# Placing the DVE and ACT code of a softmax kernel at the start of a 128-instruction block

## The chip, the cores and the metric

The kernel runs on one core of one Trainium2 chip. The metric is the device time of one execution in microseconds (us), given as the median of several. The *span* of a profile, from the first to the last instruction of the core, is 1.8 to 1.9 us shorter than that time. Engines: DVE is VectorE, ACT is ScalarE, POOL is GpSimd, PE is TensorE, SP is SyncE.

## The reference

A softmax with a temperature over rows of 1024 numbers, 32 x 512 of them, in float32:

```python
def reference(x, temperature):                     # x: 32 x 512 x 1024, temperature 0.5
    scaled = x / temperature
    shifted = scaled - np.max(scaled, axis=-1, keepdims=True)
    exp_x = np.exp(shifted)
    return (exp_x / np.sum(exp_x, axis=-1, keepdims=True)).astype(np.float32)
```

67.11 MB are read and 67.11 MB written.

## The kernel before

Sixteen tiles of 4 MB (128 partitions x 8 rows) pass through six buffers, in place. SP issues the loads, ACT the stores. A tile is worked on in two groups of four rows: DVE takes the maximum, ACT the exponential with the sum, DVE the reciprocal and four multiplications.

```python
TILES = [[8]] * 16
BUFS = 6
GROUP = 4
...
    def load():
        ...
            nc.sync.dma_start(out=xt, in_=dram(xf, i))
    def maximum(g):
        ...
        nc.vector.tensor_reduce(out=top, in_=tiles[i][:, a : a + k, :], ..., op=extreme)
        nc.vector.tensor_scalar_mul(bias, in0=top, scalar1=-scale)
    def exponential(g):
        ...
        for b in range(k):
            nc.scalar.activation(..., Exp, bias=bias[:, b : b + 1], scale=scale,
                                 accum_out=sums[:, b : b + 1])
    def divide(g):
        ...
        nc.vector.reciprocal(recip, sums)
        for b in range(k):
            nc.vector.tensor_scalar_mul(...)
    def store(g):
        ...
            nc.scalar.dma_start(out=dram(of, i)[:, a : a + k, :], in_=...)
...
    with tc.manual_schedule():
        for _ in range(BUFS):
            load()
        for g in range(len(groups) + 1):
            if g < len(groups):
                maximum(g)
                exponential(g)
            if g > 0:
                divide(g - 1)
                store(g - 1)
```

## Time and profile before

| | before |
|---|---|
| time, median (lowest to highest) | 318.26 us (317.97 to 318.32) in the first three runs |
| span of the profile | 316.0 us |
| DVE, ACT busy | 235.5 us, 149.6 us |
| loads, stores: share of the 16 DMA engines' time | 49.7%, 49.2% |
| instruction packets after the first load | 4, of 8192 bytes |

The prediction below reads the main views. Two notes help to follow it. First, the profile shows an engine's instructions being brought in by DMA, as a queue of kind "instruction" (q14 here, with the four packets of 8192 bytes of the table). In the DMA view of a short window, each line of which gives queue, packets, MB and share of the 16 engines' time, a fetch of instructions can be found by narrowing the window. This is the kernel before from 60 to 70 us, and then from 236 to 242 us:

```profile
q10 hardware_dynamic: 73, 2.39, 55.4%
q1 hardware_dynamic: 79, 2.06, 48.5%
q14 instruction: 2, 0.02, 0.4%
...
q10 hardware_dynamic: 47, 1.54, 59.4%
q1 hardware_dynamic: 43, 1.05, 41.1%
q14 instruction: 1, 0.01, 0.3%
```

The two data queues fill the DMA engines (103.9% and 100.5% in these windows); the instruction packets, few and small, stand in the same line as they do.

Second, the trace holds a record of each DMA packet with its start and duration, though not with the DMA engine that moved it. The engine can be recovered: under load a packet starts 3 to 4 ns before the recorded end of the one before it on the same engine, so the packets can be joined into 16 chains. This is worked out from the trace and not a view of the profile. A few chains can't be told apart where two packets end within some nanoseconds; I name a chain's end below only where the chain has its full 256 data packets, 128 loads and 128 stores. Here is one fetch of the kernel before in its chain (start and end in us from the span's start):

```
store packet  63.781 to 64.994   1.213 us
instructions  64.991 to 65.300   0.309 us   (8192 bytes)
load packet   65.297 to 66.972   1.675 us   (an ordinary one takes 1.213)
```

### The profile page before, as it was taken

What the parts mean: (1) busy time and instruction counts of PE and PEld (TensorE: products, weight loads), DVE (VectorE), ACT (ScalarE), POOL (GpSimd) and SP (SyncE); (2) the same over time, 40 slices, a digit from 0 to 9 for tenths busy, and PEclk for the clock granted to TensorE, in tenths of its full rate; (3) what the DMA queues carried; (4) which work ended last, traced back from release to release, by engine and by line L of the source; (5) the groups of instructions that cost most, each with busy time, mean ns of one, the idle gap of its engine ahead of it and who ended that gap; (6) DMA issues with size and microseconds to landing.
All of it is one profiled execution on the core that took longest, in us unless ns stands there. A gap on an engine that the chain in (4) does not pass through costs nothing.

```text
span 316.0 us, 620 instructions
## 1 busy us (share of the span) xinstructions
DVE 235.5 (75%) x224; ACT 149.6 (47%) x257; POOL 0.2 (0%) x4
## 2 busy tenths in 40 slices
DVE  0399999999689494994949859497693976949720
ACT  0176666666526255361554605546064560645500
POOL 0000000000000000000000000000000000000000
DMA  8999999999999999999999999999999999999996
GB/s 332 411 452 423 373 460 415 452 425 431 436 427 440 427 444 423 444 419 448 415 452 411 452 408 456 423 444 427 436 431 432 440 423 444 419 444 419 452 411 274
DMA packets 4612, 134.25 MB, mean 425 GB/s; under 512 B 512, under 2 KB 512, under 8 KB 512
## 3 DMA queue, kind: packets, MB, share of 16 engines
q1 hardware_dynamic: 2304, 67.11, 49.7%
q10 hardware_dynamic: 2304, 67.11, 49.2%
q14 instruction: 4, 0.03, 0.0%
HBM read 67.11 MB, written 67.11 MB: 425 GB/s over the span
## 4 chain that ended last, share of the span: by engine, by line
DVE 49%; DMA 32%; another core or an unknown queue 9%; ACT 5%; issue 1%; DVEq 0%; SPq 0%
DVE top L70 29%; DMA xt<-in_x_dram 20%; DVE xt L93 18%; DMA out_dram<-xt 12%; ACT xt L79 5%; DVE recip L91 1%; DVE bias L73 1%; DVEq L147 0%; SPq L61 0%
## 5 line engine op out<-in xcount | busy, mean ns | idle before, releaser
L79 ACT ACTIVATE xt<-xt,bias 128x1024 f32<-128x1024 f32 x128 | 145.4, 1137 | 136.8 <-DVE recip L91 119.4
L70 DVE TENSOR_REDUCE top<-xt 128x4 f32<-128x4096 f32 x32 | 141.3, 4416 | 62.6 <-DMA xt<-in_x_dram 62.6
L93 DVE TENSOR_SCALAR xt<-xt,recip 128x1024 f32<-128x1024 f32 x128 | 87.7, 749 | 1.1
L79 ACT ACTIVATION_READ_ACCUMULATOR xt<-xt,bias 128x1 f32 x128 | 23.9, 187 | 0.0
L79 ACT ACT_TABLE_LOAD x1 | 1.3, 1283 | 13.0 <-DMA xt<-in_x_dram 13.0
L91 DVE RECIPROCAL recip<-sums 128x4 f32<-128x4 f32 x32 | 5.5, 171 | 2.1 <-ACT xt L79 2.1
L73 DVE TENSOR_SCALAR bias<-top 128x4 f32<-128x4 f32 x32 | 5.4, 170 | 1.1
L133 POOL MEMSET const-bfloat16-1.0<- 128x1 bf16 x1 | 0.1, 101 | 0.0
L133 POOL MEMSET const-uint8-127<- 128x1 uint8 x1 | 0.1, 101 | 0.0
L133 POOL MEMSET const-float32-0.0<- 128x1 f32 x1 | 0.1, 98 | 0.2 <-issue 0.2
L133 POOL MEMSET const-float32-1.0<- 128x1 f32 x1 | 0.1, 98 | 0.0
## 6 DMA issues: line engine op xcount, KB each, us to landing
xt<-in_x_dram SPq DMA_DIRECT2D x16, 4096.0 KB, 50.2
out_dram<-xt ACTq DMA_DIRECT2D x16, 4096.0 KB, 38.6
```

Source lines behind the costliest of these rows:

```text
L70: nc.vector.tensor_reduce(out=top, in_=tiles[i][:, a : a + k, :], axis=mybir.AxisListType.X, op=extreme)
L73: nc.vector.tensor_scalar_mul(bias, in0=top, scalar1=-scale)
L79: nc.scalar.activation(tiles[i][:, a + b, :], tiles[i][:, a + b, :], mybir.ActivationFunctionType.Exp, bias=bias[:, b : b + 1], scale=scal ...
L91: nc.vector.reciprocal(recip, sums)
L93: nc.vector.tensor_scalar_mul(tiles[i][:, a + b, :], in0=tiles[i][:, a + b, :], scalar1=recip[:, b : b + 1])
L133: nc = _bacc.Bacc("TRN2", target_bir_lowering=False, num_devices=1)
```

## The change

Two directives ahead of everything else. They ask that the next DVE instruction, and the next ACT instruction, be placed on a boundary of 128 instruction slots. As no filler instructions are allowed, the padding is branched over. The intent is that the code of a tile loop does not lie across block boundaries in an arbitrary way, so that instruction fetches come at chosen places.

```diff
     with tc.manual_schedule():
+
+        nc.vector.addr_align(128, offset=0, max_nops=0)
+        nc.scalar.addr_align(128, offset=0, max_nops=0)
         for _ in range(BUFS):
             load()
```

## The prediction

Where the recorded text says what no trace of this case shows, it is cut and the cut is marked. No term of its sum is cut. The sum is 0 for the branch, 0 for stalls in the body and -0.15 us for the fetches (the middle between 0.1 worse and 0.4 better, from the packet records), so 318.26 - 0.15 = 318.1 us. The 0 for the branch rests on what is left there: DVE and ACT wait for the first load until 12.96 and 13.01 us in any case. The block of 128 instructions was an estimate, from the 127 that ACT had started between two fetches. The cost under rival (c) was a guess.

> **What bounds the kernel now.** I read the page first: the engines' totals, the slices, the queues. Then the waits, the chain of waits, the timeline at the first load and in the steady part, and last the DMA view of short windows, because the change can act only on how DVE and ACT get their instructions.
>
> ```profile
> DVE 235.5 (75%) x224; ACT 149.6 (47%) x257; POOL 0.2 (0%) x4
> ...
> DMA  8999999999999999999999999999999999999996
> ...
> q1 hardware_dynamic: 2304, 67.11, 49.7%
> q10 hardware_dynamic: 2304, 67.11, 49.2%
> q14 instruction: 4, 0.03, 0.0%
> ```
>
> DVE is busy for 75% of the span and ACT for 47%. The 16 DMA engines read 9 tenths or more in every slice but the first and the last: loads (q1) take 49.7% and stores (q10) 49.2% of their time, 98.9% together. The records of single packets give the floor: nearly every data packet has 32 KB and takes 1.213 us. 4096 of them over 16 engines are 256 for each, so 256 x 1.213 = 310.5 us. The first data packet starts at 1.74 us and the last ends at 314.80 us. So of the 316.0 us, 310.5 are the transfers themselves, 1.7 the start, 1.2 the end, and some 2.5 are lost in between.
>
> The kernel's engines wait for this traffic:
>
> ```profile
> DVE top L70 <- DMA xt<-in_x_dram: 62.6, 12, 13.0
> ...
> SPq L61 <- DMA out_dram<-xt: 224.5, 10, 53.8
> ```
>
> DVE waits 12 times for a load, 62.6 us in all: 13.0 for the first, 3.8 to 5.1 for each later one. The load queue in turn waits ten times for a store to free a buffer. Loads of 4 MB land 19.36 us apart and so do the stores; per 19.36 us each DMA engine moves 8 packets in and 8 out, 16 x 1.213 = 19.4 us. The chain of waits gives DVE 49% and DMA 32%, which seems to say that DVE bounds the kernel. It does not: in the steady part the chain passes through a DVE that has just waited, and I decide by the equality of 19.36 and 19.4.
>
> How much room a DVE delay has, in one line of the timeline:
>
> ```profile
> 224.14 4.42 DVE L70 TENSOR_REDUCE top<-xt 128x4 f32<-128x4096 f32 x1 [4.50 <-DMA xt<-in_x_dram]
> 243.90 4.42 DVE L70 TENSOR_REDUCE top<-xt 128x4 f32<-128x4096 f32 x1 [4.88 <-DMA xt<-in_x_dram]
> ```
>
> In brackets stands the idle time before the instruction and what ended it. An ordinary wait is 4.5 us. The second is longer by 0.4 us; it holds one of the four fetches of q14. In the packet records these (8192 bytes, 0.31 us each) start at 64.99, 65.02, 181.93 and 240.13 us. The load landings agree: 19.36 us apart, but 19.84, 19.83 and 19.74 where those fetches lie.
>
> [...] ACT had started 67 instructions at 65.0 us and 194 at 181.9, so 127 lie between two fetches. I therefore take 128 as the block, as the change does. [...] the load packets beside the four fetches took 1.68, 1.75, 1.48 and 1.75 us where all others in the steady part took 1.21. A fetch is free for DVE and ACT but costs one DMA engine 0.3 to 0.5 us. [...]
>
> **The change part by part.** Removed: nothing. The instruction order of the changed kernel is the same on all five engines except for one alignment directive ahead of the first DVE and the first ACT instruction. Added: padding up to the next boundary of 128 slots; as no filler instructions are allowed, I expect it to be branched over.
>
> Step 1, the branch. It comes once on each engine at about 0.7 us, after the starting barrier. The timeline shows what the engines then do:
>
> ```profile
> 0.73 57.16 SPq L61 DMA_DIRECT2D xt<-in_x_dram  x7
> 12.96 4.42 DVE L70 TENSOR_REDUCE top<-xt 128x4 f32<-128x4096 f32 x1 [12.96 <-DMA xt<-in_x_dram]
> 13.01 1.28 ACT L79 ACT_TABLE_LOAD   x1 [13.01 <-DMA xt<-in_x_dram]
> ```
>
> They wait until 12.96 and 13.01 us for the first load, which SP issues at 0.73 us without asking either. [...] Cost on the path: 0.
>
> Step 2, stalls removed in the body. There are none to remove. DVE's only gaps over 0.3 us after the first load are eleven waits for loads and one of 1.9 us for ACT in the last group. ACT waits for DVE's results. No gap is a fetch. Gain: 0.
>
> Step 3, the number of fetches under load. DVE's body is 224 arithmetic instructions and 10 semaphore waits, 234; begun at slot 0 it meets one boundary, at 128. ACT's is 128 activations, 128 accumulator reads, one table load, 16 stores and 40 waits, 313: boundaries at 128 and 256. Before, each met two (DVE had started 47 at 65.0 and 186 at 240.1[...]). So three mid-run fetches instead of four, perhaps with one for each engine at the start, when the first load is beginning.
>
> Step 4, what a fetch costs the end. The fetches of ACT and those of DVE seem to delay two different DMA engines: in the last store fourteen finish their last data packet by 313.82 us, one at 314.42 and one at 314.80. The end is set by the later one, which carries two fetches; I take it, without proof, to be DVE's (its two packets were lengthened by about 0.5 each). With one fetch fewer it ends near 314.3, and the other, still with two, near 314.4. Gain up to 0.4 us. If each engine also fetches at the start under load, plus 0.3 to 0.5, so from 0.1 worse to 0.4 better. Sum of the steps: 0 + 0 - 0.15, with 0.5 either way. 318.26 - 0.15 gives 318.1 us.
>
> **The rivals.** (a) A missing target at the start: [...] the first DVE and ACT instructions wait for a fetch behind the load packets. For it: a fetch under load took longer before, 0.5 us for those ahead of the span, and one queued behind several packets of 1.2 to 2 us could take some microseconds. Against it: 12.2 us of idle time. It would need more than 12 us to show, and DVE has spare time to catch up later; result 318.3. (b) Alignment removes all fetch traffic or puts it in a harmless place: at best both late DMA engines end with the others, near 313.8, a gain of 1.0 us, 317.2. The body of ACT has 313 instructions and can't avoid two boundaries[...], so I give this one chance in ten. (c) More fetches, for both ends: the padding pushes the tail and the closing barrier over another boundary, and a block is missing while everything waits. The trace has a fetch at 316.96 us, just after the span, so the tail's position does matter to it. The time reported is 2.3 us longer than the span and may include such waits. It would cost about 0.5 to 1.5 us, 318.8 to 319.8; one chance in ten. (d) A fetch that hits a moment with no spare time: between 13 and 77 us DVE works without a break (63.2 us busy of 64), and in the last group ACT and DVE alternate up to the last store. A late block there would be a real stall[...]. But stores queued up by then keep the DMA engines busy until the last one: it is issued at 302.38 us while the one before it ends near 304.6. So 2.2 us of such a stall at the end is hidden too.
>
> **Range and chances.** A gain of 2% would be 6.4 us. All time that is not the 310.5 us of transfers is 318.26 - 310.5 = 7.8 us, most of it start and end that the change does not touch, so faster by 2% is all but excluded. Slower by 2% needs a stall of over 12 us at the start or a different rate of the DMA engines, for which nothing speaks. The three runs before spread over 0.35 us. With the 0.5 us of step 4 and the smaller chances of (b) and (c) I set the range at 317.4 to 319.0. Chances: faster 0.01, within 2% 0.975, slower 0.015.
>
> **What would show it right or wrong.** Right: DVE and ACT busy times within 0.5 us of 235.5 and 149.6, DMA slices as before, first reduction still near 13.0, loads 19.36 us apart. Step 3: q14 with three packets after the first load, none near 65 us, one near 120 and one near 240 us for ACT (interpolated from 67 and 194 started) and one near 165 to 170 us for DVE. Step 4: the last data packet of the last store ends at 314.3 to 314.9. Wrong: a DVE gap that no load and no ACT instruction ends, a first reduction well after 13 us, or a longer time between the last store's end and the span's end. The step I trust least is the fourth.

## The result

The changed kernel takes 317.66 us (317.42 to 317.99, six runs), the kernel before 318.09 us (317.96 to 318.32, six runs beside it). The ratio is 0.9986, with a 95% interval from 0.9973 to 0.9999. A ratio here is the mean time of one kernel's fast runs over that of the other's of the same rounds, so not quite the ratio of the medians quoted. It is the same time within 2%: 0.4 us shorter, with an interval that just excludes 1.

The page of the changed kernel: busy time of the engines, the slices of the span, and the DMA queues (packets, MB, share of 16 engines).

```profile
DVE 235.5 (75%) x224; ACT 149.6 (47%) x257; POOL 0.2 (0%) x4
...
DMA  8999999999999999999999999999999999999996
...
q1 hardware_dynamic: 2304, 67.11, 49.7%
q10 hardware_dynamic: 2304, 67.11, 49.2%
q14 instruction: 5, 0.04, 0.0%
```

Nothing in the work has moved; only the instruction queue has five packets instead of four. The waits (engine and line waited for, us in total, times, longest) agree:

```profile
DVE top L70 <- DMA xt<-in_x_dram: 62.2, 12, 13.4
...
SPq L61 <- DMA out_dram<-xt: 224.7, 10, 53.6
```

The timeline of the changed kernel at its start, and at the three load waits that matter (start us, duration us, instruction; in brackets the idle time before it):

```profile
0.73 2.89 SPq L61 DMA_DIRECT2D xt<-in_x_dram  x6
13.42 4.42 DVE L70 TENSOR_REDUCE top<-xt 128x4 f32<-128x4096 f32 x1 [13.42 <-DMA xt<-in_x_dram]
13.47 1.28 ACT L79 ACT_TABLE_LOAD   x1 [13.47 <-DMA xt<-in_x_dram]
...
87.96 4.42 DVE L70 TENSOR_REDUCE top<-xt 128x4 f32<-128x4096 f32 x1 [3.16 <-DMA xt<-in_x_dram]
...
166.13 4.42 DVE L70 TENSOR_REDUCE top<-xt 128x4 f32<-128x4096 f32 x1 [5.21 <-DMA xt<-in_x_dram]
...
204.83 4.42 DVE L70 TENSOR_REDUCE top<-xt 128x4 f32<-128x4096 f32 x1 [4.47 <-DMA xt<-in_x_dram]
```

Three things are to be seen. DVE's first reduction starts 0.45 us later than before (13.42 against 12.96 us). That delay is gone by 88 us: the first wait for a load in the steady part, 3.78 us before the change,

```profile
88.13 4.42 DVE L70 TENSOR_REDUCE top<-xt 128x4 f32<-128x4096 f32 x1 [3.78 <-DMA xt<-in_x_dram]
```

is shorter by 0.6 us, and this reduction starts 0.17 us earlier than before. And one wait, the one ahead of 166.13 us, is longer than an ordinary one (4.47 us in the last line) by 0.7 us: it is the one with DVE's fetch in it. The packet records give the places of all fetches after the span's start, and the end of the last data packet:

```
before:   64.99   65.02   181.93   240.13                (316.96, after the work)   last data 314.80
changed:   1.76    3.60   124.63   162.34   253.33                                  last data 314.47
```

Where the branch is, the view of its line shows it (line, engine, operation and count: duration in ns, start in us):

```profile
L109 DVEq COMPARE_BRANCH  x1: 47/47/47, 0.8 to 0.8; - x1
```

In this pair of profiles most of the time went from the end of the data traffic: the last data packet ends 0.33 us earlier and the span is 0.36 us shorter, while the two profiled executions differ by 0.44 us (317.86 and 317.42). The rest lies outside the span, which accounts for 1.87 us of the time before and 1.78 us after. It goes with the fetch at 316.96 us, which is gone: on the mean of its runs every kernel here that keeps that fetch has 1.85 to 1.90 us outside the span, and each of the five without it (the changed kernel, e2, e3, e6, e8) has 1.75 to 1.80 us. With a spread of 0.36 to 0.57 us within each kernel's runs, one pair of profiles does not prove where the time went; hence the experiments.

### The profile page after: what moved, and what is told of

The parts are those of the page before. It is cut to its first block, busy times and chain, and to the rows that moved or that the text cites. A ratio compares the mean times of both kernels' runs of the same rounds, so it can differ in the third digit from the quotient of the medians.

```text
span 315.6 us, 622 instructions
## 1 busy us (share of the span) xinstructions
DVE 235.5 (75%) x224; ACT 149.6 (47%) x257; POOL 0.2 (0%) x4
## 4 chain that ended last, share of the span: by engine, by line
DVE 72%; another core or an unknown queue 15%; DMA 4%; ACT 3%; issue 1%; DVEq 0%
DVE top L70 43%; DVE xt L93 27%; DMA xt<-in_x_dram 4%; ACT xt L79 3%; DVE recip L91 1%; DVE bias L73 1%; DVEq L150 0%
```

## The experiments

**Theory.** A fetch of instructions stalls neither DVE nor ACT (no gap of theirs over 0.3 us in the kernel before is put down to one), but it takes a place in the queue of one DMA engine. Each instruction stream has its own such DMA engine (in the kernel before two chains end late, at 314.42 and 314.80 us). Loads and stores are split over all 16 (128 packets of each to a chain), so a tile has landed only when the latest of them is done, and the kernel ends when the latest has moved its last store packet. **Rivals**: the gain is noise; it comes from ACT's placing or from the branch; the total number of fetches counts and not the latest DMA engine; a fetch is free unless an engine waits for it.

### One directive alone, and both again (e1, e2, e3)

```diff
# e1, from the changed kernel: DVE only
-        nc.scalar.addr_align(128, offset=0, max_nops=0)
# e2, from the changed kernel: ACT only
-        nc.vector.addr_align(128, offset=0, max_nops=0)
```

e3 is the changed kernel unaltered. Expected of e1:

> Theory (lateness of single DMA engines): the fetches of DVE and of ACT fall on two different DMA engines, and the later one sets the end; before, that was DVE's, with last data at 314.80 us against 314.42 for the other. With DVE alone aligned, its mid-run fetches go from two (65, 240 us) to one (near 162), plus one at the start; ACT's stay near 65 and 182. Last data near 314.4 us, ratio 0.9980 to 0.9995. Rival 1 (the measured 0.9986 is noise or chip drift): 0.9993 to 1.0007. Rival 2 (the gain comes from where ACT's fetches fall): 1.000.

Of e2:

> Theory: ACT's fetches move to near 124 and 253 us plus one at the start, DVE's stay near 65 and 240 us and still set the end at 314.8 us; ratio 0.9995 to 1.0015. Rival 1 (noise): 0.9993 to 1.0007. Rival 2 (the gain is ACT's): 0.998 to 0.999.

Of e3:

> The changed kernel once more, as control on the same chip as the two halves. Theory: ratio 0.9973 to 0.9995, five fetches at the same places as in its first profile (1.8, 3.6, near 124, 162, 253 us). Rival 1 (noise): the interval holds 1.0 and the ratio is nearer to 1 than 0.9995.

Measured, five runs each, beside nine runs of the kernel before (317.95 us):

| | time, us | ratio to before (95%) | DVE's fetches, us | its DMA engine's last data | ACT's fetches, us | its DMA engine's last data |
|---|---|---|---|---|---|---|
| before (nine runs; places of the first profile) | 317.95 | 1 | 65.0, 240.1 | 314.80 | 65.0, 181.9 | 314.42 |
| e1, DVE only | 317.54 | 0.9990 (0.9977 to 1.0004) | 3.8, 162.3 | 314.44 | 63.8, 182.9 | 314.13 |
| e2, ACT only | 317.83 | 0.9999 (0.9986 to 1.0011) | 65.0, 240.1 | 314.76 | 1.8, 123.5, 252.3 | 314.65 |
| e3, both | 317.66 | 0.9989 (0.9977 to 1.0002) | 3.8, 162.4 | 314.55 | 1.8, 123.5, 252.3 | 314.69 |

The two chains that carry instruction packets are the two latest in all four profiles; the others end at 314.03 us at the latest. Moving one directive moves just one of the two streams, which tells which is which: the later one in the kernel before, at 314.80, is DVE's, as the prediction had taken it without proof. e1 has nearly the whole gain, e2 none, as the theory said; the rival that the gain is ACT's falls. (e2 does save time outside the span, 1.75 us on the mean of its runs against 1.90 before, but its mean span is not shorter, 316.20 us against 316.09.) The intervals of e1 and e3 taken alone still include 1.0, so none of these runs alone excludes noise.

A finding in the table was not expected: ACT's directive makes its own DMA engine *later*, 314.65 and 314.69 against 314.42. The likely reason, not tested alone, is the fetch that it adds at the start to two that remain. In e3 it is ACT's DMA engine that ends last. Its last data packet also comes 0.22 us later than that of the first profile of the same kernel (314.47), so a single profile's tail is uncertain by about as much as the differences in the last columns.

### A large dose of fetches on an idle engine (e4)

Half a microsecond in 318 is hard to see; twenty fetches are not. GpSimd does nothing in this kernel but four small fills at the start. Filling it with empty instructions should bring fetches and nothing else; in the page of e4 the packets of the data queues are as many as before and DVE and ACT are busy for 235.7 and 149.6 us.

```diff
     with tc.manual_schedule():
+        for _ in range(2560):
+            nc.gpsimd.nop(nofuse=True, hint="filler")
```

> The kernel before with 2560 empty instructions on the idle GpSimd, which takes part in nothing: 20 blocks of 128, so about 20 fetches of 8192 bytes more. Theory (each fetch under load delays the DMA engine that carries it, and the end waits for the latest one): 20 x 0.31 to 20 x 0.5 us, so 6 to 10 us longer, 324 to 328 us, with one DMA engine far behind the other fifteen at the end. Rival (fetches spread over the DMA engines or fit in gaps): under 1 us longer. Rival (only fetches that an engine waits for cost anything): 0.

Measured: 329.88 us (329.36 to 330.29, four runs) against 317.95, ratio 1.0373 (1.0359 to 1.0387). Its DMA queues:

```profile
q1 hardware_dynamic: 2304, 67.11, 47.9%
q10 hardware_dynamic: 2304, 67.11, 47.5%
q14 instruction: 24, 0.20, 0.1%
```

Twenty packets more than the four of before, one for each 128 of the 2560 instructions and 0.1% of the DMA engines' time, cost 11.93 us, 0.60 us each. The empty instructions themselves, 0.04 us apart, paused at every 128th, for 0.3 to 0.6 us in most cases and once each for 1.6 and 3.1 us. The timeline shows where it comes out: the first reduction of the last tile, first in the kernel before, then in e4.

```profile
282.62 4.42 DVE L70 TENSOR_REDUCE top<-xt 128x4 f32<-128x4096 f32 x1 [4.50 <-DMA xt<-in_x_dram]
```

```profile
296.75 4.42 DVE L70 TENSOR_REDUCE top<-xt 128x4 f32<-128x4096 f32 x1 [4.58 <-DMA xt<-in_x_dram]
```

The last load landed 14 us later. The packet records show when the delay builds up: loads land some 11.0 us apart at the start (9.7 before) and 20.5 to 22.1 us apart (16.5 to 19.8 before) while GpSimd's fetches come, up to 116 us, and after them 19.4 to 19.6 us apart (19.4 to 19.8 before). One chain carries all twenty fetches, and at the end the other DMA engines stand idle for 9.0 to 9.8 us from 295.4 to 296.1 us on: they have delivered their parts, and no further store can be issued before DVE has worked on that load. So a share averaged over 16 engines (0.1%) says nothing of a cost that falls on one of them. The theory's estimate of 6 to 10 us was too low, because it put a fetch at 0.3 to 0.5 us. The rivals, under 1 us and 0, fall.

### The dose split, halved, and with a partner (e5, e9, e10)

```diff
# e5, from the kernel before: split
+        for _ in range(1280):
+            nc.gpsimd.nop(nofuse=True, hint="filler")
+            nc.tensor.nop(nofuse=True, hint="filler")
# e9, from the kernel before: half
+        for _ in range(1280):
+            nc.gpsimd.nop(nofuse=True, hint="filler")
# e10, from e9: SP as well
         for _ in range(BUFS):
             load()
+        for _ in range(1024):
+            nc.sync.nop(nofuse=True, hint="filler")
```

Expected of e5:

> The same 2560 empty instructions on the kernel before, but 1280 on GpSimd and 1280 on TensorE, both idle otherwise. 2560 on GpSimd alone cost 11.9 us, 0.60 us for each of the 20 fetches, all on one DMA engine. Theory (the end waits for the latest DMA engine; each instruction stream has its own): 10 fetches on each of two DMA engines, so 10 x 0.60 = 6 us longer, 323 to 325 us. Rival (the total number of fetches counts, whichever engine carries them): 12 us longer, near 330 us. Theory with both streams on one DMA engine: also 330, and the packet records would show it.

Of e9:

> The kernel before with 1280 empty instructions on GpSimd alone. In the split run TensorE's 1280 brought no fetch at all within the span, so it was a half dose (10 fetches on one DMA engine) without a partner; it cost 7.9 us on the mean, with runs from 6.0 to 9.2. Theory: 10 fetches cost 6 to 8 us, 324 to 326 us.

Of e10:

> The half dose on GpSimd, and 1024 empty instructions on SP between its sixth and seventh load (SP stands waiting there until 57 us), some 8 more fetches on another DMA engine. Theory (the latest DMA engine sets the end): as the half dose alone on this chip, within 1.5 us. Rival (the total number of fetches counts): 8 x 0.6 to 8 x 0.8, 5 to 6.5 us longer than the half dose. If SP's fetches fall on GpSimd's DMA engine, also that much longer, and the packet records show it.

Measured against the runs of before on the same chip:

| | time, us | longer by, us | fetches within the span besides the kernel's four |
|---|---|---|---|
| e4, POOL 2560 | 329.88 | 11.93 | 20 of 8 KB |
| e9, POOL 1280 | 323.66 | 5.64 | 10 of 8 KB |
| e10, POOL 1280 and SP 1024 | 324.18 | 6.16 | 10 + 8 of 8 KB |
| e5, POOL 1280 and PE 1280 | 326.25 (323.96 to 327.14) | 8.22 | 10 of 8 KB, 5 of 16 KB |

The half dose costs half: 0.56 us for each fetch. Here are the instruction queue of e9 and then of e10:

```profile
q14 instruction: 14, 0.11, 0.1%
...
q14 instruction: 22, 0.18, 0.1%
```

Eight more fetches on SP's DMA engine cost 0.5 us, not the 4.5 us (8 x 0.56) that counting all fetches would ask for. The latest DMA engine counts, not the sum. The packet records put SP's fetches into another chain than GpSimd's.

e5 was meant to show the same and does so less clearly. I first read it as a half dose, because I had listed q14 alone; the text for e9 repeats that error. The page of e5 shows that PE's instructions came by a queue of their own:

```profile
q8 instruction: 5, 0.08, 0.1%
q14 instruction: 14, 0.11, 0.1%
```

These are five packets of 16384 bytes, one for each 256 of PE's 1280 instructions (POOL's 1280 came in ten of 8192), of 0.88 to 0.98 us each, and the load packets that followed three of them took 1.63 to 1.71 us, 0.46 us more than 1.213 on the mean. An estimate from these records is 5 x (0.92 + 0.46) = 6.9 us for PE's DMA engine, more than the 5.6 us of GpSimd's ten. The maximum of the two is 6.9, the sum 12.5; measured were 8.2 (median). This is on the side of the maximum, but 1.3 us is left. Its runs spread from 323.96 to 327.14 us, and its profile has slow packets on many DMA engines near 212 us that I can't explain. It is left open.

### Another place in the block (e6, e11)

```diff
# e6, from the changed kernel: both at slot 100
-        nc.vector.addr_align(128, offset=0, max_nops=0)
-        nc.scalar.addr_align(128, offset=0, max_nops=0)
+        nc.vector.addr_align(128, offset=100, max_nops=0)
+        nc.scalar.addr_align(128, offset=100, max_nops=0)
# e11, from the changed kernel: DVE alone at slot 100
-        nc.vector.addr_align(128, offset=0, max_nops=0)
-        nc.scalar.addr_align(128, offset=0, max_nops=0)
+        nc.vector.addr_align(128, offset=100, max_nops=0)
```

Expected of e6:

> The changed kernel with both directives at offset 100 in place of 0: ACT's body begins 28 slots ahead of a boundary and then meets boundaries at 28, 156 and 284 of its 313, DVE's at 28 and 156 of its 234. Theory: ACT's DMA engine carries three mid-run fetches and one at the start, against two and one in the changed kernel, so its last data comes 0.4 to 0.8 us later, near 315.1 us; ratio to before 1.000 to 1.002, and 0.4 to 0.8 us slower than the changed kernel. Rival (being aligned or entering by a branch is what helps, not the number of fetches): ratio 0.9985 to 0.9995 as the changed kernel.

Measured: 317.79 us (317.71 to 318.15) against 318.03, ratio 0.9992 (0.9980 to 1.0005). My expectation, ACT's DMA engine later by 0.4 to 0.8 us than in the changed kernel, did not come true; the number of the rival did. The trace shows why the experiment did not separate them. It has no fetch at the start, although both engines execute the branch. Slot 100 is in the block in which the engines already are (e8 below shows 61 slots of padding up to the boundary, so they stand at slot 67 of 128), and no boundary is crossed. ACT's three fetches, 38.3, 155.0 and 279.0 us, are as many as in the changed kernel (one early, two late), and DVE's, 34.3 and 201.3 us, too. With equal numbers the theory expects equal times. The latest chains end at 314.72 (ACT's) and 314.70 us (DVE's), the time is not to be told from the changed kernel's. What the run does show is that the branch alone brings no fetch up to 30 us; where a boundary is crossed, as in the changed kernel, fetches come at 1.76 and 3.60 us. Here are ACT's branch and, of the DMA view from 0 to 30 us, the queues, in which the instruction queue is missing:

```profile
L110 ACTq COMPARE_BRANCH  x1: 41/41/41, 0.7 to 0.7; - x1
...
q1 hardware_dynamic: 400, 12.06, 95.3%
```

From e1, e2 and e6 follows a candidate: keep ACT where it was, with two late fetches and no third, and place DVE so that its body crosses one boundary early and one late. Expected of e11:

> A candidate: DVE alone aligned, at offset 100, so that its first boundary comes after 28 instructions (near 38 us, when all DMA engines are slowed by the first store anyway) and its second at 156 (near 200 us), none later; ACT as in the kernel before. Theory: last data at 314.2 to 314.7 us, ratio 0.998 to 0.9995, at best 0.3 us better than the changed kernel, not to be told from it by these runs. Rival (only offset 0 with a branch helps): 1.000.

Measured: 317.31 us (317.28 to 317.61, five runs) against 318.02, ratio 0.9981 (0.9968 to 0.9993). DVE's fetches fell at 34.0 and 200.8 us and ACT's at 64.9 and 181.6. (The slowing near the first store, which the expectation names, stands in the packet records of the kernel before: that store is issued at 32.66 us, and 28 load packets that start from 33.9 to 35.9 us take 1.27 to 2.60 us in place of 1.213.) The latest data packet of all ends at 314.24 us, ACT's chain at 314.06. This is the best of all runs, and its interval excludes 1.0. It was compared with the kernel before, not with the changed kernel on the same chip. Each of the changed kernel's two ratios (0.9986, 0.9989) lies inside its interval, so that it beats the changed kernel is likely but not shown. DVE's two fetches lie at the same places in e6 and e11, yet its DMA engine ends at 314.70 us in the one profile and at 314.24 in the other. So the fetches of a DMA engine do not fix its end in one profile to better than half a microsecond, and what e11 shows rests on its five times.

### A late DVE (e7)

The first rival of the prediction was a stall at the start, with room for about 12 us. This run delays DVE by work that fetches nothing.

```diff
     with tc.manual_schedule():
+        idle = ctx.enter_context(tc.tile_pool(name="idle", bufs=1)).tile([P, 1024], f32, name="idle")
+        for _ in range(24):
+            nc.vector.memset(idle, 0.0)
```

> The kernel before, with 24 fills of a scrap tile ahead of DVE's first reduction, so that DVE begins some 10 to 14 us later than the first load's landing near 13 us. Asks how long a stall at the start could be before it shows: the prediction's first rival put the limit at about 12 us. Theory (six buffers of loads keep the DMA engines busy until near 58 us without any DVE, and DVE waits for loads after 84 us): no change, within 0.6 us of before. Rival (the start is on the path once DVE is later than the first load): 10 to 14 us longer.

Measured: 318.59 us (318.43 to 318.74) against 318.03, 0.56 us more, ratio 1.0016. In its timeline DVE starts 16.3 us later than before, further than I had planned. The second line is from its waits:

```profile
29.25 4.36 DVE L70 TENSOR_REDUCE top<-xt 128x4 f32<-128x4096 f32 x1
...
DVE top L70 <- DMA xt<-in_x_dram: 23.0, 6, 4.5
```

DVE's waits for loads shrank from 62.6 us to 23.0 us. It caught up from its idle time, while six buffers of loads kept the DMA engines at work (an estimate from the packets of the kernel before: 6 loads of 8 packets for each DMA engine, 48 x 1.213 = 58.2 us). A delay at the start of 16 us shows as 0.56 us at the end; the rival that asked for 10 to 14 us falls.

### Filler instead of the branch (e8)

```diff
-        nc.vector.addr_align(128, offset=0, max_nops=0)
-        nc.scalar.addr_align(128, offset=0, max_nops=0)
+        nc.vector.addr_align(128, offset=0, max_nops=127)
+        nc.scalar.addr_align(128, offset=0, max_nops=127)
```

> The changed kernel with up to 127 empty filler instructions allowed, so the padding is run through in place of a branch over it; the body lies in the same slots. Theory (only where the fetches fall counts): the same five fetches, ratio 0.998 to 0.9995 as the changed kernel, no compare-and-branch on DVE and ACT at 0.7 us. Rival (the branch itself, and the fetch after it, make the difference): ratio 0.9995 to 1.0005.

Measured: 317.87 us (317.66 to 317.93) against 318.03, ratio 0.9992 (0.9979 to 1.0004). Five fetches as in the changed kernel (7.3 and 7.5 us in place of 1.8 and 3.6, then 123.6, 162.6 and 252.5). The ratio is inside the range that the theory gave, but so near its edge, and so near the rival's range, that the time does not decide. The trace gives three other things. First, the changed kernel's places did not bring its early end: the last data packet, ACT's, ends at 314.83 us and DVE's at 314.67, so the three profiles of these places (314.47, 314.69, 314.83) run from 0.33 us ahead of the kernel before (314.80) to level with it. Second, the branch is gone, and its line shows what replaced it:

```profile
L109 DVEq NOP  x61: 18/18/18, 0.8 to 3.6; - x61
```

So 61 slots of padding lay ahead of DVE's body (and 61 ahead of ACT's): in the kernel before, both bodies began 61 slots short of a boundary. That gives boundaries after 61 and 189 of DVE's 234 instructions and after 61 and 189 of ACT's 313 (the third would come after 317), two late fetches each, just as found. Third, the first fetches, at 7.3 and 7.5 us, came after the engines had run through the padding to the boundary (its last instructions start at 3.6 us on DVE and 3.1 us on ACT), with no branch at all. In these runs entering a new block is followed by a fetch, by a branch (1.76 and 3.60 us in the changed kernel) or by running into it; which block it brings was not shown.

## Why the prediction was right

The predicted time was 318.1 us, measured were 317.66, inside the range of 317.4 to 319.0, and the class was right. By its own steps:

1. *The branch costs nothing on the path.* Right. It took 0.047 us on DVE and 0.033 us on ACT (0.041 in e2 and e6). The prediction also said that the first reduction would stay near 13.0 us; it came at 13.42, and at 13.6 to 13.7 in e1, e3 and e8, where DVE fetches at the start too, while ACT's fetch alone (e2) left it at 13.0. DVE's early fetch seems to hold up a part of the first load. For DVE that is harmless, since in e7 a start 16.3 us later cost 0.56 us.
2. *No stall to remove.* Right: the busy times and the kinds of wait are those of before.
3. *The number and places of the fetches.* Right in all five: three mid-run, at 124.6 and 253.3 us for ACT (predicted near 120 and 240) and 162.3 us for DVE (165 to 170), one for each engine at the start, none near 65 us. It rests on the block of 128 instructions, which e4 bears out (20 fetches for 2560).
4. *What a fetch costs the end*, the step trusted least. The mechanism was right: two DMA engines, in the kernel before the later being DVE's, and the later one sets the end (e1, e2, and with large doses e9, e10). The last data packet, predicted at 314.3 to 314.9 us, came at 314.47, 314.69 and 314.83 in the three profiles of these places. The size of one term was off. The prediction read the lengthening of the following load packet as the whole cost, 0.3 to 0.5 us. The fetch's own 0.31 us comes on top: the four fetches of the kernel before, each with the lengthening of the packet behind it, come to 0.58 to 0.84 us, and the dose gave 0.56 to 0.60 us. The sum was still close, because the second DMA engine, ACT's, was only 0.38 us behind the first in the kernel before, and its directive adds a fetch. However large DVE's gain, ACT's DMA engine, at 314.65 us in e2, 314.69 in e3 and 314.83 in e8, then holds up the end. That the mis-sized term made so little difference is luck, and so is a part of the gain: some 0.1 us of it lies outside the span, where the prediction had looked only for harm, as rival (c).

Of the rivals, (a) did not happen, and past its limit of about 12 us most of a delay is still hidden: 16.3 us showed as 0.56 us (e7). (b) did not happen; e11 goes some of the way. (c), a cost in the tail, did not happen: the fetch at 316.96 us is ACT's (it is there in all runs that leave ACT in its old place, and in none that aligns ACT), it is absent in the changed kernel, and the time outside the span fell, from 1.87 us to 1.78 us in the profiled runs. (d) did not happen.

Three readings in the prediction were off without bearing on its result. The 2.3 us between time and span set the median of all runs against the span of a faster one; within the profiled run it is 1.87 us. The fetches of 0.5 us named as being under load came ahead of the span, before the first load packet; the four of that profile under load took 0.31 us each. And the store before the last ended at 305.1 us on the latest DMA engine, not near 304.6.

What is open: the exact share of the changed kernel's 0.4 us that comes from DVE's fetch alone, as the interval barely excludes 1. Five ratios of kernels with DVE's body moved to one late fetch and nothing else added to the work (0.9986, 0.9990, 0.9989, 0.9992 and 0.9981; e6 gave 0.9992 too) are all below 1, and the one with only ACT moved is 0.9999. That pattern supports the theory more than any of them alone, though the changed kernel, e3, e6 and e8 also have the 0.1 us (0.0003 of the time) outside the span; e1 and e11 do not. How much of so small a gain is due to the number of fetches, to their places or to the scatter of single DMA engines is argued, not shown. What the large doses show is that fetches on one DMA engine delay the whole kernel and that the latest DMA engine counts.

## What to carry to other kernels

When the DMA engines are the bound, ask of every small transfer which single DMA engine carries it and whether that one is the last to finish; an average over 16 engines hides it (0.1% in e4). Aligning code moved instruction fetches to other places and dropped one or two of them, worth 0.1 to 0.2% of the time at the most, while long runs of instructions on an idle engine cost more than they seem to (20 fetches, 11.9 us). A delay at the start of an engine that later waits for loads was nearly free here (16.3 us cost 0.56 us), so look for such waits before spending effort there.
